# Softmax attention: biased scores moved from PSUM to rows in SBUF, one exponential for a token tile, and another split of the PSUM banks

## The chip, the cores and the metric

The kernel runs on one core of one Trainium2 chip. The metric is the device time of one execution in microseconds (us), the median over runs. Five engines matter: TensorE (PE in the profile; PEld is its weight load), VectorE (DVE), ScalarE (ACT), GpSimd (POOL) and SyncE (SP, which only issues DMAs). PE writes its results into PSUM, which has eight banks of 128 x 512 four-byte values; DVE and ACT read and write PSUM and SBUF.

## The reference, cut to what matters

A network of two layers. Each layer normalises its input, multiplies it with one wide matrix, and gives part of the columns to gated linear attention (GLA, four heads) and part to softmax attention with a forget gate (FoX, eight heads of width 64). The two outputs are normalised by head, joined, multiplied by an output matrix and added to the input; a gated feed-forward network with a short convolution follows. Sequence: 16 learned tokens and 1024 others, 1040 in all. All is float32. FoX is what the change touches:

```python
c = jnp.cumsum(log_f, axis=1)
logits = (jnp.einsum('bqhd,bkhd->bhqk', q_b, kf)
          + c_b[..., None] - c_k[:, :, None, :])
logits = jnp.where(key_pos[None, :] <= q_pos[:, None], logits, -jnp.inf)
return jnp.einsum('bhqk,bkhd->bqhd', jax.nn.softmax(logits, axis=-1), vf)
...
o_fox = rms_norm(o_fox, fox_norm[i].reshape(FOX_HEADS, FOX_DH)).reshape(B, L, FOX_WIDTH)
h = h + jnp.concatenate([o_gla, o_fox], axis=-1) @ w_out[i]
```

## The kernel before

**Numbers in two halves.** Matrix products of full precision are made of three products of a short format: each operand is split into `hi` (a cast on ACT) and `lo` (the rest, a subtraction on DVE, or on POOL for weights). So each product of a layer's weights appears as `mm<-xh,hi`, `mm<-xh,lo`, `mm<-xl,hi` (L221 to L223), and `split` (L332) is an ACT cast at L335 followed by a DVE subtraction at L336.

**FoX.** The 1040 tokens make nine token tiles: tile 0 of 112 tokens, the others of 116. The eight heads are worked through as four pairs p, two heads e in each; for each pair the tiles come in five groups (7,8), (5,6), (3,4), (1,2), (0), for each group both heads, for each head the later tile first. That gives 72 steps in a layer. A step's work for one token tile i and one head is:

- `fox_scores` (L642): the keys up to the tile's end come in chunks of 460, 464 and 116 (`SCORES`). For each chunk PE makes the scores into a PSUM tile `S` by two matmuls (L657, L658). DVE adds the bias row `cb` in place in PSUM and keeps a running minimum `m` (the instruction and its read of the accumulator, both L660; the sign is turned, so that the minimum is the softmax's maximum). When all chunks are there, ACT makes the exponential of each chunk from PSUM into an SBUF tile `P` (`Ps` for the third chunk) at L672, with a sum by row into `d3`; DVE adds the sums to `den` (L676).
- `fox_transposes` (L679), two steps later: PE transposes P tile by tile, up to four into one PSUM tile `tr` (L693; for the third chunk into a bank of `S`, L686), and `split` brings it to SBUF as `PT`, hi and lo. `PT0`, `PT1` and `PT2` stand for the three chunks; there is one buffer of each.
- `fox_av`, three steps later: PE multiplies values by `PT` into the PSUM tile `av` (L711), which ACT copies to SBUF (L714, `avs`).
- `fox_fold` (L716), four steps later: PE transposes `avs` into `fo`, a bank of `S` (L724). ACT and DVE add hi and lo to `ff` (L727, L728), ACT squares it into the SBUF tile `fon` (L730), DVE sums the squares (L734) and multiplies the rows by the inverse root (L739).
- `fox_store` (L743), six steps later: PE transposes the result into a bank of `S` (L750); ACT scales it to SBUF (L757), from where a DMA takes it away. For the last pair it is split into the operand of the output product.

Between these PE runs fill work: the products of the next pair's queries, keys and values, and gates, one accumulator (`mm`) after the other, with ACT and DVE work behind it (L571 to L630). In the last pair the fill work is the output product of the layer.

**Order.** Each engine runs one list in order. A scheduler sets the lists from the source's order, priorities (scores come with a priority of 8) and estimated times; an instruction that waits holds all behind it on its engine. PSUM banks are given out by tag, in turn: `mm` 2, `S` 3, `tr` 2, `av` 1 (L875). A bank is given to the next user of its tag when the last reader of the one before is through.

`head` (L352) makes a layer's first products before anything else fills `mm`; its five accumulators go in turn to the tags `mm, mm, S, S, S` (L355).

Of the kernel before, what the change touches and what calls it, by code (L numbers as in the profile page):

```python
# [10 lines left out]
F32 = mybir.dt.float32  # L11
F32R = mybir.dt.float32r
BF16 = mybir.dt.bfloat16
AF = mybir.ActivationFunctionType
# [22 lines left out]
P_BUFS = 5  # L37
# [97 lines left out]
class Kern:  # L135
# [216 lines left out]
    def head(self, tiles, pp, nm, feed):  # L352
        s = self.slots
        held, w, waiting = [], [], []
        tags = ("mm", "mm", "S", "S", "S")  # L355
        i = 0
# [285 lines left out]
    def fox_scores(self, e, i, q, cb, den, ap, pp):  # L642


        nc = self.nc
        rows = self.rows_of(i)
        kend = self.start_of(i) + rows
        qs = slice(kend - rows, kend)
        m = ap.tile([128, 3], F32, tag="m", name="m", bufs=4)
        Ss = []  # L650
        for c0, n in SCORES:
            if c0 >= kend:
                break
            k1 = min(c0 + n, kend)
            n = k1 - c0
            S = pp.tile([128, 512], F32, tag="S", name="S")
            nc.tensor.matmul(S[:rows, :n], q["qA"][e][:, qs], q["kA"][e][:, c0:k1], start=True, stop=False)  # L657
            nc.tensor.matmul(S[:rows, :n], q["qA"][e][:, qs], q["kL"][e][:, c0:k1], start=False, stop=True)  # L658
            ci = len(Ss)
            nc.vector.tensor_tensor_reduce(out=S[:rows, :n], in0=S[:rows, :n], in1=cb[:rows, c0:k1],  # L660
                                           scale=1.0, scalar=(BIG if ci == 0 else m[:rows, ci - 1:ci]),
                                           op0=ALU.add, op1=ALU.min, accum_out=m[:rows, ci:ci + 1])
            Ss.append((S, n))
        nch = len(Ss)
        Ps = []
        d3 = den if nch == 1 else ap.tile([128, 3], F32, tag="d3", name="d3", bufs=4)
        for ci, (S, n) in enumerate(Ss):
            if ci < 2:
                P = ap.tile([128, 4 * FT], F32, tag="P", name="P", bufs=P_BUFS)
            else:  # L670
                P = ap.tile([FT, FT], F32, tag="Ps", name="Ps", bufs=2)
            nc.scalar.activation(P[:rows, :n], S[:rows, :n], AF.Exp, scale=-1.0, bias=m[:rows, nch - 1:nch],  # L672
                                 accum_out=(den if nch == 1 else d3[:rows, ci:ci + 1]))
            Ps.append(P)
        if nch > 1:
            nc.vector.tensor_reduce(out=den, in_=d3[:rows, :nch], axis=AX.X, op=ALU.add)  # L676
        return Ps

    def fox_transposes(self, i, ci, P, PT, qoff, pp):  # L679
# [3 lines left out]
        tr = pp.tile([128, 4, 128], F32, tag="S" if ci == 2 else "tr", name="tr")  # L683
# [6 lines left out]
        for j in range(nt):  # L690
            t = 4 * ci + j
            o, w = self.start_of(t) - self.start_of(4 * ci), FT if i else FIRST
            nc.tensor.transpose(tr[:w, j, :rows], P[:rows, o:o + w], id_)  # L693
# [22 lines left out]
    def fox_fold(self, tiles, avs, den, ap, pp):  # L716
# [3 lines left out]
        fo = pp.tile([128, 2, 2, 2, 64], F32, tag="S", name="fo")  # L720
# [8 lines left out]
        on = sq = ap.tile([128, 2, 2, 64], F32, tag="fon", name="fon", bufs=1)  # L729
        nc.scalar.activation(sq[:rows, :nt], f[:rows, :nt], AF.Square)  # L730
        vv, d2, y0, a = (ap.tile([128, 2, 2], F32, tag=f"f{x}", name=f"f{x}", bufs=2)[:rows, :nt] for x in "vdya")
# [9 lines left out]
        return on  # L741
# [961 lines left out]
```

## Time and profile before

| what | value |
|---|---|
| three runs | 2593.61, 2605.56, 2600.95 us (median 2600.95) |
| span of the profiled execution | 2598.6 us |
| busy: PE / DVE / ACT / POOL | 2505.2 / 1782.3 / 1281.9 / 430.0 us |
| share of the span | 96% / 69% / 49% / 17% |
| FoX stage of layer 0, of layer 1 | about 181 to 530 us, about 1458 to 1820 us |
| exponentials L672 into P, into Ps | 224 and 16 instructions |
| scores L660 on DVE | 240 instructions and 240 reads of the accumulator |

The profiled execution has no time of its own beside its span; the span is what the profile's windows add up to. Times inside the trace are counted from the span's start. A row of waits reads: who waited, for whom, in total (us), how often, the longest. A row of the timeline reads: start, duration, engine, line, operation, output and inputs, shape, and in brackets the idle time before it with what ended it. A row of windows reads: stretch, length, busy time and count of PE, PEld, DVE, ACT and POOL, then the granted clock of PE (1.00 is full), the share of DMA and the rate.

### The profile page before, as it was taken

How to read it: one execution, taken by the hardware profiler on the slowest of the kernel's cores; microseconds unless marked ns; L12 is line 12 of the kernel's file. 1: busy time of each engine (PE TensorE's matmuls, PEld its weight loads, DVE VectorE, ACT ScalarE, POOL GpSimd, SP SyncE). 2: the span in 40 equal slices, each digit the busy share in tenths (PEclk: the TensorE clock that was granted, in tenths of full speed). 3: DMA queues.
4: the chain of work that ended last, by engine and by line, in shares of the span. 5: the costliest groups of instructions: out<-in, count | busy, mean ns of one | idle time of the engine just before them, and what ended most of it. 6: DMA issues, size and time to landing. Idle time of an engine off the chain costs nothing.

```text
span 2598.6 us, 48715 instructions
## 1 busy us (share of the span) xinstructions
PE 2505.2 (96%) x19278; PEld 2432.4 (94%) x19278; DVE 1782.3 (69%) x3486; ACT 1281.9 (49%) x2737; POOL 430.0 (17%) x598
## 2 busy tenths in 40 slices
PE   8999999899999999999999999998999999999997
PEld 7988999898999999999999899997999999999997
DVE  7656776759877777853665666776698777777535
ACT  7336666535544445641443466665454444455312
POOL 4033334310000000100201233332100000001002
PEclk9999999999999999999999999999999999999999
DMA  3132134333322223763312222142523222247621
GB/s 125 66 86 57 54 93 127 103 121 100 110 75 82 79 82 129 198 160 113 106 53 66 72 78 71 61 142 91 157 62 115 82 78 74 85 157 185 188 66 69
DMA packets 118517, 260.93 MB, mean 100 GB/s; under 512 B 14880, under 2 KB 32544, under 8 KB 118288
## 3 DMA queue, kind: packets, MB, share of 16 engines
q1 hardware_dynamic: 93984, 182.79, 22.4%
q0 software_dynamic: 22432, 72.71, 10.1%
q8 instruction: 151, 2.47, 0.4%
q10 hardware_dynamic: 1872, 2.31, 0.3%
q14 instruction: 78, 0.64, 0.1%
HBM read 177.16 MB, written 67.81 MB: 94 GB/s over the span
## 4 chain that ended last, share of the span: by engine, by line
PE 60%; issue 17%; DVE 14%; ACT 5%; DMA 2%; POOL 1%; SPq 0%; DVEq 0%; POOLq 0%; ACTq 0%
PE mm L221 6%; PE mm L222 6%; PE mm L223 6%; PE up L221 5%; PE up L223 5%; PE up L222 5%; PE down L221 5%; PE down L222 5%; PE down L223 5%; PE av L711 2%; DVE S L660 2%; PE tr L693 2%; ACT P L672 1%; DVE PT L336 1%; PE S L657 1%
## 5 line engine op out<-in xcount | busy, mean ns | idle before, releaser
L221 PE MATMUL up<-x,hi 128*128 128x260 f32 (+1 forms) x2464 | 700.0, 284 | 2.4 <-ACT x L1050 2.4
L223 PE MATMUL up<-x,hi 128*128 128x260 f32 (+1 forms) x2464 | 698.9, 284 | 1.9 <-DVE x L1051 1.8
L222 PE MATMUL up<-x,lo 128*128 128x260 f32 (+1 forms) x2464 | 698.6, 284 | 0.0
L223 PEld LDWEIGHTS up<-x,hi 128*128 128x128 f32 x2464 | 468.2, 190 | 3.4 <-DVE x L1051 3.4
L221 PEld LDWEIGHTS up<-x,hi 128*128 128x128 f32 x2464 | 467.4, 190 | 3.5 <-ACT x L1050 3.2
L222 PEld LDWEIGHTS up<-x,lo 128*128 128x128 f32 x2464 | 467.5, 190 | 0.2 <-DVE lo L1027 0.2
L1027 DVE TENSOR_TENSOR lo<-raw,hi 128x512 fp32r<-128x512 f32 x364 | 248.8, 688 | 171.8 <-ACT hi L1026 171.8
L221 PE MATMUL mm<-xh,hi 128*128 128x348 f32 (+4 forms) x1056 | 365.5, 346 | 0.0
L223 PE MATMUL mm<-xl,hi 128*128 128x348 f32 (+4 forms) x1056 | 341.3, 323 | 0.0
L222 PE MATMUL mm<-xh,lo 128*128 128x348 f32 (+4 forms) x1056 | 340.1, 322 | 0.0
L1026 ACT CAST hi<-raw 128x512 fp32r<-128x512 f32 x364 | 224.4, 621 | 138.5 <-PE up L223 93.5
L221 PEld LDWEIGHTS mm<-xh,hi 128*128 128x128 f32 x1056 | 201.0, 190 | 5.8 <-issue 5.3
L188 ACT CAST hi<-raw 128x512 fp32r<-128x512 f32 (+2 forms) x184 | 107.4, 587 | 200.7 <-PE down L223 116.2
L222 PEld LDWEIGHTS mm<-xh,lo 128*128 128x128 f32 x1056 | 200.9, 190 | 0.4 <-issue 0.3
L223 PEld LDWEIGHTS mm<-xl,hi 128*128 128x128 f32 x1056 | 199.8, 189 | 0.3 <-issue 0.3
L222 PE MATMUL down<-ah,lo 128*128 128x260 f32 (+1 forms) x704 | 198.6, 282 | 0.4 <-DVE lo L190 0.3
L223 PE MATMUL down<-al,hi 128*128 128x260 f32 (+1 forms) x704 | 198.4, 282 | 0.0
L221 PE MATMUL down<-ah,hi 128*128 128x260 f32 (+1 forms) x704 | 198.1, 281 | 0.0
L672 ACT ACTIVATE P<-S,m 116x460 f32<-116x460 f32 (+2 forms) x224 | 124.8, 561 | 103.9 <-DVE m L660 101.5
L336 DVE TENSOR_TENSOR PT<-tr,PT 116x464 fp32r<-116x464 f32 (+3 forms) x240 | 123.0, 516 | 63.8 <-ACT PT L335 62.9
L1235 POOL DMA_DIRECT2D actd<-cv x44 | 23.6, 536 | 763.7 <-DVE cv L1234 742.8
L1009 DVE TENSOR_TENSOR raw<-raw,raw 128x512 f32<-128x512 f32 x198 | 129.8, 689 | 19.7 <-DMA raw<-in_wd_dram 17.2
(277 smaller groups left out, 5889.6 us busy)
## 6 DMA issues: line engine op xcount, KB each, us to landing
raw<-in_wm_dram SPq DMA_DIRECT2D x330, 256.0 KB, 2.8
raw<-in_wd_dram SPq DMA_DIRECT2D x64, 256.0 KB, 3.5
actd<-cv POOLq DMA_DIRECT2D x22, 520.0 KB, 3.0
actd<-cv POOLq DMA_DIRECT2D x22, 512.0 KB, 3.0
cb<-cd SPq DMA_DIRECT2D x16, 520.0 KB, 4.0
st<-actd SPq DMA_DIRECT2D x14, 520.0 KB, 4.6
st<-actd SPq DMA_DIRECT2D x14, 512.0 KB, 5.2
kA<-kA SPq DMA_DIRECT2D x24, 260.0 KB, 4.3
```

The source lines that it names most:

```text
L188: nc.scalar.copy(hi[:, :n, :], raw[:, :n, :])
L221: nc.tensor.matmul(ps, wh, xh[:, c0:c0 + n], start=first, stop=False, skip_group_check=more)
L222: nc.tensor.matmul(ps, wl, xh[:, c0:c0 + n], start=False, stop=False, skip_group_check=more)
L223: nc.tensor.matmul(ps, wh, xl[:, c0:c0 + n], start=False, stop=last, skip_group_check=more)
L336: nc.vector.tensor_tensor(out=lo, in0=src, in1=hi.bitcast(F32), op=ALU.subtract)
L660: nc.vector.tensor_tensor_reduce(out=S[:rows, :n], in0=S[:rows, :n], in1=cb[:rows, c0:k1], scale=1.0, scalar=(BIG if ci == 0 else m[:rows, ...
L672: nc.scalar.activation(P[:rows, :n], S[:rows, :n], AF.Exp, scale=-1.0, bias=m[:rows, nch - 1:nch], accum_out=(den if nch == 1 else d3[:row ...
L693: nc.tensor.transpose(tr[:w, j, :rows], P[:rows, o:o + w], id_)
L711: nc.tensor.matmul(av[:, a:width], w.rearrange("p a b -> p (a b)"), x, start=(t == 0 and i == 0), stop=(t == last and i == 1))
L1009: nc.vector.tensor_tensor(out=q[out][:, :nk, :], in0=q[a][:, :nk, :], in1=q[b][:, :nk, :], op=op)
L1026: nc.scalar.copy(hi[:, :nk, :], src[:, :nk, :])
L1027: nc.vector.tensor_tensor(out=lo[:, :nk, :], in0=src[:, :nk, :], in1=hi[:, :nk, :].bitcast(F32), op=ALU.subtract)
```

## The change

DVE now writes the biased scores of a chunk not back to PSUM but into a row in SBUF: `P` is one tile of 924 columns (`LOW`) for the first two chunks, `Ps` one of 116 for the third. ACT then makes one exponential in place over the row's first part, at most 924 wide, and one over `Ps` where there is one. Sums of two parts are added by one DVE instruction, only for rows of three chunks. A bank of `S` is free once DVE is through, and no longer once ACT is. The tags have other banks: `S` 2 in place of 3, `tr` 3 in place of 2. `fo`, the transposes of `fox_store` and those of `Ps` take a bank of `tr` in place of one of `S`; `head` takes its five accumulators in the order `mm, S, mm, S, tr`. The squares go to the half of `fo`'s bank that has been read, and the product with the inverse root is made in place in `ff`, so that the tile `fon` is gone. Line numbers after the change are one or two higher.

```diff
-P_BUFS = 5
+LOW = 924
+P_BUFS = 3
...
-        tags = ("mm", "mm", "S", "S", "S")
+        tags = ("mm", "S", "mm", "S", "tr")
...
-            nc.vector.tensor_tensor_reduce(out=S[:rows, :n], in0=S[:rows, :n], in1=cb[:rows, c0:k1],
+            ci = len(Ps)
+            if ci == 0:
+                P = ap.tile([128, LOW], F32, tag="P", name="P", bufs=P_BUFS)
+            elif ci == 2:
+                P = ap.tile([FT, FT], F32, tag="Ps", name="Ps", bufs=2)
+            x = P[:rows, c0:k1] if ci < 2 else P[:rows, :n]
+            nc.vector.tensor_tensor_reduce(out=x, in0=S[:rows, :n], in1=cb[:rows, c0:k1],
                                            scale=1.0, scalar=(BIG if ci == 0 else m[:rows, ci - 1:ci]),
                                            op0=ALU.add, op1=ALU.min, accum_out=m[:rows, ci:ci + 1])
-            Ss.append((S, n))
-        nch = len(Ss)
-        Ps = []
-        d3 = den if nch == 1 else ap.tile([128, 3], F32, tag="d3", name="d3", bufs=4)
-        for ci, (S, n) in enumerate(Ss):
-            if ci < 2:
-                P = ap.tile([128, 4 * FT], F32, tag="P", name="P", bufs=P_BUFS)
-            else:
-                P = ap.tile([FT, FT], F32, tag="Ps", name="Ps", bufs=2)
-            nc.scalar.activation(P[:rows, :n], S[:rows, :n], AF.Exp, scale=-1.0, bias=m[:rows, nch - 1:nch],
-                                 accum_out=(den if nch == 1 else d3[:rows, ci:ci + 1]))
             Ps.append(P)
-        if nch > 1:
-            nc.vector.tensor_reduce(out=den, in_=d3[:rows, :nch], axis=AX.X, op=ALU.add)
+        nch = len(Ps)
+        low = m[:rows, nch - 1:nch]
+        d2 = ap.tile([128, 2], F32, tag="d2", name="d2", bufs=2) if nch == 3 else None
+        x = Ps[0][:rows, :min(kend, LOW)]
+        nc.scalar.activation(x, x, AF.Exp, scale=-1.0, bias=low, accum_out=(den if nch < 3 else d2[:rows, 0:1]))
+        if nch == 3:
+            x = Ps[2][:rows, :rows]
+            nc.scalar.activation(x, x, AF.Exp, scale=-1.0, bias=low, accum_out=d2[:rows, 1:2])
+            nc.vector.tensor_tensor(out=den, in0=d2[:rows, 0:1], in1=d2[:rows, 1:2], op=ALU.add)
...
-        tr = pp.tile([128, 4, 128], F32, tag="S" if ci == 2 else "tr", name="tr")
+        tr = pp.tile([128, 4, 128], F32, tag="tr", name="tr")
...
-        fo = pp.tile([128, 2, 2, 2, 64], F32, tag="S", name="fo")
+        fo = pp.tile([128, 2, 2, 2, 64], F32, tag="tr", name="fo")
...
-        on = sq = ap.tile([128, 2, 2, 64], F32, tag="fon", name="fon", bufs=1)
+        sq = fo[:, :, :, 0]
...
-            nc.vector.tensor_tensor(out=on[:rows, ti], in0=f[:rows, ti],
+            nc.vector.tensor_tensor(out=f[:rows, ti], in0=f[:rows, ti],
...
-        tr = pp.tile([128, 4, 128], F32, tag="S", name="tr")
+        tr = pp.tile([128, 4, 128], F32, tag="tr", name="tr")
...
-            pp = PsumTags({"mm": (pp2, 2), "S": (pp1, 3), "tr": (pp2, 2), "av": (pp1, 1)})
+            pp = PsumTags({"mm": (pp2, 2), "S": (pp1, 2), "tr": (pp2, 3), "av": (pp1, 1)})
```

The scheduler makes new lists out of this. In most places a list reads as before and only what is waited for differs. Three places follow; the prediction calls them A, B and C. All three are in layer 0, pair 1, and recur in the other pairs. The bracket at a row's end names the engine whose semaphore the row waits for; what it stands for is told with each. `kA`, `kL` and `qA` are the keys (hi, lo) and the queries of a head.

**Place A**, PE, the first row of a pair, with its three chunks. Before:

```order
L657 MATMUL S<-kA_2370,qA_2368 116x460 [waits DMAHW1_49]
L693 MATMUL tr<-ident,P 112x112 [waits PE_49]
L658 MATMUL S<-kL_2372,qA_2368 116x460 [waits DMAHW3_49]
L657 MATMUL S<-kA_2370,qA_2368 116x464
L658 MATMUL S<-kL_2372,qA_2368 116x464 [waits Pool_49]
L657 MATMUL S<-kA_2370,qA_2368 116x116 [waits Activation_49]
L658 MATMUL S<-kL_2372,qA_2368 116x116
L221 MATMUL mm<-xh_138,hi 128x344
L222 MATMUL mm<-xh_138,lo 128x344
L223 MATMUL mm<-xl_139,hi 128x344
```

And after the change:

```order
L658 MATMUL S<-kA_2358,qA_2356 116x460 [waits DMAHW1_49]
L695 MATMUL tr<-ident,P 112x112 [waits PE_49]
L659 MATMUL S<-kL_2360,qA_2356 116x460 [waits DMAHW3_49]
L658 MATMUL S<-kA_2358,qA_2356 116x464
L659 MATMUL S<-kL_2360,qA_2356 116x464 [waits Pool_49]
L222 MATMUL mm<-xh_138,hi 128x344
L223 MATMUL mm<-xh_138,lo 128x344
L224 MATMUL mm<-xl_139,hi 128x344
L658 MATMUL S<-kA_2358,qA_2356 116x116 [waits DVE_49]
L659 MATMUL S<-kL_2360,qA_2356 116x116
```

The third chunk's matmul has moved behind three `mm`. It waited for ACT to be through with a bank that `fox_store` had used; it now waits for DVE to be through with the first chunk of the same row, the one just made, since there are two banks.

**Place B**, PE, the second row of tile group (5,6). Before:

```order
L657 MATMUL S<-kA_2370,qA_2368 116x460 [waits Activation_49]
L222 MATMUL mm<-xh_142,lo 128x344
L658 MATMUL S<-kL_2372,qA_2368 116x460
L223 MATMUL mm<-xl_143,hi 128x344
L693 MATMUL tr<-ident,P 116x116 [waits DVE_49]
L657 MATMUL S<-kA_2370,qA_2368 116x232 [waits Activation_49]
```

And after the change:

```order
L658 MATMUL S<-kA_2358,qA_2356 116x460 [waits DVE_49]
L223 MATMUL mm<-xh_142,lo 128x344
L659 MATMUL S<-kL_2360,qA_2356 116x460
L224 MATMUL mm<-xl_143,hi 128x344
L695 MATMUL tr<-ident,P 116x116 [waits DVE_49]
L658 MATMUL S<-kA_2358,qA_2356 116x232
```

The order stands. The first `S` waited for the exponential of the row before (its first chunk); it now waits for DVE's bias instruction on that chunk. The `tr` waits in both for the DVE subtraction that makes `PT0` out of the `tr` bank it takes. On ACT, at the same place, before:

```order
L623 ACTIVATE gy<-gy 128x348
L335 CAST PT_3572<-tr 116x4x116
L672 ACTIVATE P,d_3592<-S,m 116x460
L672 ACTIVATE P,d_3592<-S,m 116x348
L335 CAST PT_3573<-tr 116x4x116
L714 COPY avs<-av 128x232
```

And after the change:

```order
L624 ACTIVATE gy<-gy 128x348
L336 CAST PT_3519<-tr 116x4x116
L674 ACTIVATE P,den<-P,m 116x808
L336 CAST PT_3520<-tr 116x4x116
L716 COPY avs<-av 128x232
```

The exponential over 460 and the one over 348 stand as one over 808, between the same two casts.

**Place C**, PE, the second row of tile group (1,2). Before:

```order
L223 MATMUL mm<-xl_147,hi 128x348
L657 MATMUL S<-kA_2370,qA_2368 116x228 [waits Activation_49]
L658 MATMUL S<-kL_2372,qA_2368 116x228
L693 MATMUL tr<-ident,P 116x116 [waits DVE_49]
L693 MATMUL tr<-ident,P 116x116 x3
L221 MATMUL mm<-xh_132,hi 128x344
```

And after the change:

```order
L224 MATMUL mm<-xl_147,hi 128x348
L658 MATMUL S<-kA_2358,qA_2356 116x228
L659 MATMUL S<-kL_2360,qA_2356 116x228
L695 MATMUL tr<-ident,P 116x116 [waits DVE_49,PE_49]
L695 MATMUL tr<-ident,P 116x116 x3
L222 MATMUL mm<-xh_132,hi 128x344
```

The order stands here too. `S` has no wait left. The first `tr` waited for the DVE subtraction that empties the `tr` bank of two uses before into `PT0`; with three banks it takes the bank that `fo` had, and waits for DVE's sum of squares (L734 before, L736 after).

More of the change, by code (lines that the diff above doesn't have):

```diff
@@ L649, in fox_scores @@
         m = ap.tile([128, 3], F32, tag="m", name="m", bufs=4)
-        Ss = []
+        Ps = []
         for c0, n in SCORES:
@@ L691, in fox_transposes @@
             t = 4 * ci + j
-            o, w = self.start_of(t) - self.start_of(4 * ci), FT if i else FIRST
+            o, w = self.start_of(t), FT if i else FIRST
             nc.tensor.transpose(tr[:w, j, :rows], P[:rows, o:o + w], id_)
@@ L728, in fox_fold @@
         nc.vector.tensor_tensor(out=f[:rows, :nt], in0=fo[:rows, :nt, :, 1], in1=f[:rows, :nt], op=ALU.add)
-        on = sq = ap.tile([128, 2, 2, 64], F32, tag="fon", name="fon", bufs=1)
+        sq = fo[:, :, :, 0]
         nc.scalar.activation(sq[:rows, :nt], f[:rows, :nt], AF.Square)
-        vv, d2, y0, a = (ap.tile([128, 2, 2], F32, tag=f"f{x}", name=f"f{x}", bufs=2)[:rows, :nt] for x in "vdya")
+        vv, d2, y0, a = (ap.tile([128, 2, 2], F32, tag=f"f{x}", name=f"f{x}", bufs=1)[:rows, :nt] for x in "vdya")
         nc.vector.scalar_tensor_tensor(out=d2, in0=den[:rows, :nt], scalar=64.0 * EPS,
```

3 lines of the change are left out of this document (1 added, 2 removed).

## Prediction

> **What bounds the kernel now.** I read the page first (busy time by engine, chain by engine), then windows by stage, then what PE waited for in the two stages that the change touches.
>
> ```profile
> PE 2505.2 (96%) x19278; PEld 2432.4 (94%) x19278; DVE 1782.3 (69%) x3486; ACT 1281.9 (49%) x2737; POOL 430.0 (17%) x598
> ...
> PE 60%; issue 17%; DVE 14%; ACT 5%; DMA 2%; POOL 1%; SPq 0%; DVEq 0%; POOLq 0%; ACTq 0%
> ```
>
> PE is busy for 96% of the span and carries most of the chain. The change takes no matmul away. So it can win only idle time of PE, and only where the waiting is for something that the change touches: a bank of scores or of transposes.
>
> ```profile
> 180.00:540.00 360.00, 334.97 (x2306) 318.45 (x2306) 242.09 (x750) 216.48 (x650) 124.45 (x176) 0.99 0.28 84
> ```
>
> The windows by stage give 360 - 335 = 25 us of idle PE in the stage of softmax attention of layer 0. The waits of PE say for what; the first fence is layer 0, the second the same stage of layer 1.
>
> ```profile
> PE tr L693 <- DVE PT L336: 9.2, 8, 2.2
> PE S L657 <- ACT P L672: 5.5, 5, 1.5
> PE mm L221 <- ACT hi L188: 2.9, 2, 2.7
> PE mm L222 <- POOL lo L190: 2.5, 4, 1.0
> ```
>
> ```profile
> PE tr L693 <- DVE PT L336: 7.8, 7, 2.2
> PE S L657 <- ACT P L672: 5.1, 5, 1.3
> ```
>
> Two rows are of the kind that the change acts on. A transpose waits until DVE has emptied a bank of `tr`; scores wait until ACT's exponential has emptied a bank of `S`. Together 14.7 us in layer 0 and 12.9 in layer 1, 27.6 us in all: the ceiling of what can be won, 1.06% of the time. The rows below them (weights cast by ACT, split by POOL) are left as they are.
>
> **The change part by part.**
>
> *The bias instruction on DVE writes SBUF.* 240 instructions, as many as before. The trace has none that writes this way; the nearest is the subtraction L336, which also reads PSUM and SBUF and writes SBUF.
>
> ```profile
> L660 DVE CUSTOM_DVE_ANT_0 S<-S,cb x144: 272/635/679, 188.3 to 1802.2; 116x460 f32<-116x460 f32 x96, 116x344 f32<-116x344 f32 x16, 116x228 f32<-116x228 f32 x16, 112x112 f32<-112x112 f32 x16
> ...
> L336 DVE TENSOR_TENSOR PT<-tr,PT x240: 264/631/643, 195.5 to 1809.9; 116x464 fp32r<-116x464 f32 x82, 116x348 fp32r<-116x348 f32 x16, 116x116 fp32r<-116x116 f32 x14, 112x112 fp32r<-112x112 f32 x8
> ```
>
> Minimum, median and maximum in ns: 635 for the one and 631 for the other, both mostly at 460 or 464 columns. I take no difference; the bounds are -0.05 and +0.05 us each, 12 us of DVE in all, of which little reaches PE, since DVE is busy for 242 of the 360 us.
>
> *One exponential for two.* The 240 exponentials become 160. The new one reads and writes SBUF and is up to 924 wide. The trace has ACT work from SBUF to SBUF at 348 and 1040 columns.
>
> ```profile
> L672 ACT ACTIVATE P<-S,m x224: 347/639/666, 191.4 to 1802.6; 116x460 f32<-116x460 f32 x80, 116x344 f32<-116x344 f32 x16, 116x116 f32<-116x116 f32 x8, 112x112 f32<-112x112 f32 x8
> ...
> L621 ACT ACTIVATE ge<-ge x24: 491/495/521, 265.8 to 1759.0; 128x348 f32<-128x348 f32 x16, 128x344 f32<-128x344 f32 x8
> ...
> L335 ACT CAST x<-st x24: 1037/1056/1087, 1040.8 to 2367.0; 128x1040 fp32r<-128x1040 f32 x12, 128x1024 fp32r<-128x1024 f32 x12
> ```
>
> A line through 495 ns at 348 and 1056 at 1040 rises by 0.811 ns a column: 0.868 us at 808, 0.962 at 924. The pair of exponentials over 460 and 348 (next fence) holds ACT from 285.78 until the next cast starts at 286.93, 1.15 us. The single one would hold it for about 0.87, so it saves some 0.28, and 80 of these 22 us. Bounds: nothing (if the exponential is as much dearer than a cast as 639 ns at 460 columns is against 586 on my line, 0.05 us, and its sum is read out on top) and 30 us. ACT is busy for 216 of the 360 us and is waited for by PE only through the banks, so I count none of it by itself.
>
> [...]
>
> *Place B: scores no longer wait for the exponential.* The timeline of pair 1, layer 0:
>
> ```profile
> 285.06 0.32 PE L221 MATMUL mm<-xh,hi 128*128 128x344 f32 x1
> 286.57 0.47 PE L657 MATMUL S<-kA,qA 128*116 128x460 f32 x1 [1.19 <-ACT P L672]
> ...
> 287.40 0.26 PE L693 MATMUL tr<-ident,P 116*116 116x116 f32 x1
> ...
> 285.78 0.65 ACT L672 ACTIVATE P<-S,m 116x460 f32<-116x460 f32 x1
> ...
> 286.93 0.55 ACT L335 CAST PT<-tr 116x464 fp32r<-116x464 f32 x1
> ...
> 284.64 0.14 DVE L660 DVE_READ_ACCUMULATOR2_ANT m<- 116x1 f32 x1
> ...
> 285.91 0.64 DVE L336 TENSOR_TENSOR PT<-tr,PT 116x464 fp32r<-116x464 f32 x1
> ...
> 456.14 0.47 PE L657 MATMUL S<-kA,qA 128*116 128x460 f32 x1 [1.31 <-ACT P L672]
> ```
>
> PE stood for 1.19 us until the exponential was through. DVE was through with that bank at 284.78, before PE wanted it, so this stall goes. But the `tr` three rows further waits, before and after, for the subtraction that ends at 285.91 + 0.64 = 286.55. It starts there and not at 287.40: net gain 0.85 us of 1.19. The place comes in pairs 1, 2 and 3 (the last at 456.14): 3 x 0.85 = 2.55.
>
> *Place C: a third bank of transposes.* The same pair, and the same place in pair 2:
>
> ```profile
> 325.71 0.61 PE L693 MATMUL tr<-ident,P 116*116 116x116 f32 x4 [1.36 <-DVE PT L336]
> ...
> 329.14 0.57 PE L711 MATMUL av<-PT,V 112*128 112x232 f32 x3
> ...
> 327.65 0.64 DVE L336 TENSOR_TENSOR PT<-tr,PT 116x464 fp32r<-116x464 f32 x1 [0.63 <-ACT PT L335]
> ...
> 321.18 0.42 DVE L734 TENSOR_REDUCE fv<-fon 116x4 f32<-116x256 f32 x1 [0.48 <-ACT fon L730]
> ...
> 410.35 0.32 PE L693 MATMUL tr<-ident,P 116*116 116x116 f32 x1 [1.37 <-DVE PT L336]
> ```
>
> The transposes now take the bank that `fo` had, free since the sum of squares at 321.60, so the 1.36 us go. PE would reach the next `av` at 329.14 - 1.36 = 327.78. That `av` needs `PT0`, which DVE finishes at 327.65 + 0.64 = 328.29 by a chain (exponential of 344 columns, cast, subtraction) that the change does not shorten. So `av` is late next: the gain is 329.14 - 328.29 = 0.85. Pairs 0, 1 and 2: 2.55.
>
> *Pair 3.* Here the fill work is the output product, whose operands DVE and ACT split.
>
> ```profile
> 482.64 1.95 DVE L336 TENSOR_TENSOR ml<-h,mh 128x384 fp32r<-128x384 f32 x4
> ...
> 486.30 0.63 DVE L336 TENSOR_TENSOR PT<-tr,PT 116x464 fp32r<-116x464 f32 x1
> ...
> 481.81 0.61 PE L693 MATMUL tr<-ident,P 116*116 116x116 f32 x4 [2.20 <-DVE PT L336]
> ...
> 485.07 0.41 PE L693 MATMUL tr<-ident,P 116*116 116x116 f32 x2 [1.38 <-DVE PT L336]
> ...
> 486.99 0.38 PE L711 MATMUL av<-PT,V 112*128 112x232 f32 x1 [0.33 <-DVE PT L336]
> ```
>
> The 2.20 and the 1.38 us go, but the `av` at 486.99 waited for DVE already, which works through splits without a pause. PE comes earlier to the same wait. I take 0.5 us, between nothing and their sum.
>
> *The rest of a layer*: pair 0's start and some small waits, 14.7 - 3.75 (B) - 4.1 (C) - 3.6 (pair 3), with 1.25 for B as the mean of the two rows shown, 1.37 for C, and 2.20 + 1.38 for pair 3. That leaves 3.3 us, where the order is rearranged most. I take 0.6, between -2 and +2.
>
> *Place A: a wait is added.* The third chunk's scores now wait for DVE's work on the first chunk of their own row; queued behind them on PE are the fill products and all transposes.
>
> ```profile
> 261.66 0.21 PE L657 MATMUL S<-kA,qA 128*116 128x116 f32 x1
> ...
> 261.82 0.38 PE L221 MATMUL mm<-xh,hi 128*128 128x344 f32 x1
> ...
> 262.34 0.32 PE L221 MATMUL mm<-xh,hi 128*128 128x344 f32 x1
> ...
> 261.44 0.65 DVE L660 CUSTOM_DVE_ANT_0 S<-S,cb 116x460 f32<-116x460 f32 x1 [1.11 <-PE S L658]
> 262.00 0.14 DVE L660 DVE_READ_ACCUMULATOR2_ANT m<- 116x1 f32 x1
> ```
>
> Three `mm` (261.82 to 262.34, 0.52 us) now stand ahead, so PE would come at about 261.66 + 0.52 = 262.18; DVE is through at 262.14. I cost it at nothing. The cover is 0.04 us, though: whatever delays DVE here delays PE by as much.
>
> *`fo`, stores and `Ps` in banks of `tr`, squares in PSUM, shorter sums:* nothing; their waits lie several fill products behind their producers. Bounds of -1 and +1 us a layer.
>
> Sum for a layer: 2.55 + 2.55 + 0.5 + 0.6 = 6.2 us. Layer 1 shows nearly the same waits: 12.4 us, off the profiled span of 2598.6 about 2586. The span is 2.35 us below the median of the runs shown; against the median I take the same difference: 2601 - 12 = **2589 us**.
>
> **The rivals.**
>
> *All of the waits go* (2573 us). Then `PT`'s chain would have to move ahead with PE. For it: with three banks a cast has more to choose from, and shorter exponentials let ACT come sooner. Against it: at B and C the next wait is in the trace. Price: 27.6 us, 2601 - 27.6.
>
> *The waits only change their name* (2600 us). Three more users crowd the three banks of `tr`, and `PT0`, with its one buffer, is waited for in any case. For it: 0.34 us of B and 0.5 of C come back already on paper, and pair 3 keeps nearly all. Against it: 0.85 us remain at six places. Price: 0 to 3 us gained.
>
> *Scores hold PE* (2614 us, slower). PE's list is in order. With two banks each chunk's scores need DVE to be through two chunks back, and at place A the margin is 0.04 us. If DVE has other things ahead there, say one subtraction of 0.64 us with one bias instruction of 0.63, PE stands for 1.3 us at the 16 rows with three chunks (there are 16 `Ps`), 21 us, which leaves 12.4 - 21 = 8.6 us lost. Against it: in pair 1 DVE had stood idle for 1.11 us before, waiting for PE. A pause may also cost speed:
>
> ```profile
> 180.00:184.00 4.00, 2.24 (x14) 1.78 (x14) 3.91 (x10) 1.20 (x4) 2.51 (x2) 1.00 0.19 68
> 184.00:188.00 4.00, 4.00 (x19) 3.76 (x19) 1.17 (x4) 2.03 (x7) 1.10 (x2) 0.57 0.70 217
> ...
> 324.00:328.00 4.00, 2.64 (x19) 2.46 (x19) 2.07 (x6) 3.75 (x11) 2.81 (x3) 1.00 0.04 4
> ```
>
> After 4 us with 2.24 of PE's work the granted clock was 0.57 for the next 4; after 2.64 at place C (a stall as it is now) the row has 1.00. So a stretch like the first costs (1 - 0.57) x 4 = 1.7 us more. Three or four of the 16 rows falling into it give 2601 + 8.6 + 5 = 2614. It decides from 12.4 / 16 = 0.8 us a row (no gain left) and from 25.4 / 16 = 1.6 us a row, the clock included, it is slower by over 0.5%. [...]
>
> **How the numbers follow.** Forecast (waits of B and C, less what comes back, 2582 to 2596) 0.45; all go 0.18; names only 0.22; scores hold PE 0.15. A measurement tells 0.5%, 13 us, from no change, and the forecast of 12 lies at that line: of its 0.45 I put 0.22 beyond it. Faster: 0.22 + 0.18 = 0.40. Of the slower rival 0.12 is beyond the line on the other side; the same: 0.23 + 0.22 + 0.03 = 0.48. The range runs from the ceiling of what can be won, 2573, to 2608, which cuts the slower rival's larger half.
>
> **What would show it.** Right: the row of scores waiting for the exponential is gone, transposes waiting for `PT` fall to about 4 us a layer, and `av` waiting for `PT` rises by some 2 us; idle PE in the window of 360 us falls from 25 to about 19. Wrong: waits of scores for DVE of more than 3 us a layer (rival three), `tr` waiting for `fo` or the store (rival two), or a bias instruction clearly above 0.64 us.

## The result

| kernel | median of runs | range | span of the profiled execution |
|---|---|---|---|
| before | 2603.26 us (4 runs) | 2593.61 to 2606.36 | 2598.6 us |
| changed | 2591.23 us (4 runs) | 2589.74 to 2591.80 | 2589.8 us |

The ratio is 0.9955, 95% interval 0.9934 to 0.9976: 12 us faster. That interval reaches from 6 to 17 us. The change was timed twice more, with ratios of 0.9962 (0.9950 to 0.9974) and 0.9965 (0.9953 to 0.9977), which is 9 us each time.

The page of the changed kernel, busy time and chain by engine, and the row of windows for the attention stage of layer 0 (PE busy second after the length):

```profile
PE 2503.3 (97%) x19278; PEld 2431.3 (94%) x19278; DVE 1770.5 (68%) x3422; ACT 1267.7 (49%) x2577; POOL 428.3 (17%) x598
...
PE 54%; issue 23%; DVE 12%; ACT 4%; DMA 4%; POOL 2%; SPq 0%; DVEq 0%; POOLq 0%; ACTq 0%
```

```profile
180.00:540.00 360.00, 341.42 (x2350) 325.96 (x2349) 240.03 (x728) 212.89 (x580) 123.73 (x176) 0.99 0.29 86
```

Idle PE in that window fell from 25.0 to 18.6 us. What PE waited for there (total, times, longest):

```profile
PE tr L695 <- DVE PT L337: 5.2, 5, 2.1
...
PE S L658 <- DVE m L666: 2.5, 6, 0.8
PE mm L224 <- DVE ml L337: 2.2, 2, 1.2
PE tr L545 <- DVE on L538: 1.5, 2, 1.0
...
PE av L713 <- DVE PT L337: 0.5, 2, 0.3
```

And in layer 1:

```profile
PE tr L695 <- DVE PT L337: 4.8, 5, 2.1
...
PE mm L224 <- DVE ml L337: 2.2, 2, 1.2
...
PE S L658 <- DVE m L666: 1.9, 5, 0.7
```

No scores wait for an exponential any more (5.5 and 5.1 us before). Transposes wait for 4.0 and 3.0 us less. Two rows are larger or new: scores now wait for DVE's bias instruction, 2.5 and 1.9 us, and products of the last pair wait 2.2 us for `ml`, 0.5 before.

To compare kernels whose lists differ, lengths were taken from the traces' PE records between matmuls that every kernel has: the time from the last score matmul of the pair before (the one of 112 x 112) to that of pair 1 and of pair 3, and the attention part of a layer, from its first `z` (a product of the gated linear attention) to the first `up` of the feed-forward network. The attention part thus holds the gated linear attention as well as FoX.

```
                 pair 1, layer 0 / 1     pair 3, layer 0 / 1     attention part, layer 0 / 1
before           84.23 / 84.30           94.58 / 93.20           549.95 / 548.76
before again     84.24 / 84.51           95.02 / 92.97           547.09 / 548.69
changed          82.20 / 82.14           95.85 / 93.73           541.39 / 541.80
changed again    82.34 / 82.05           95.25 / 93.04           541.00 / 541.03
changed, third   82.30 / 82.07           94.97 / 95.47           541.68 / 544.86
rows only        84.96 / 83.10           96.29 / 93.87           547.32 / 544.23
banks only       83.08 / 83.15           96.79 / 94.58           548.37 / 553.37
two exponentials 82.94 / 82.72           94.02 / 94.08           540.57 / 544.33
```

Profiles of one kernel agree to 0.2 us in pair 1, but differ by up to 2.4 us in pair 3 and by up to 3.8 in the attention part. The last section shows one cause. The mean of both layers together is 1097.2 us before (two profiles) and 1083.9 with the change (three): 13.3 us won there. The rest of the spans took a mean of 1502.1 us before and 1504.6 with the change; the two profiles of the kernel before differ by 4.4 us there, so this is no finding.

### The profile page after: what moved, and what is told of

The parts are those of the page before. It is cut to its first block, busy times and chain, and to the rows that moved or that the text cites. A ratio compares the mean times of both kernels' runs of the same rounds, so it can differ in the third digit from the quotient of the medians.

```text
span 2589.8 us, 48526 instructions
## 1 busy us (share of the span) xinstructions
PE 2503.3 (97%) x19278; PEld 2431.3 (94%) x19278; DVE 1770.5 (68%) x3422; ACT 1267.7 (49%) x2577; POOL 428.3 (17%) x598
## 4 chain that ended last, share of the span: by engine, by line
PE 54%; issue 23%; DVE 12%; ACT 4%; DMA 4%; POOL 2%; SPq 0%; DVEq 0%; POOLq 0%; ACTq 0%
PE mm L222 6%; PE mm L223 6%; PE mm L224 6%; PE down L222 5%; PE down L223 5%; PE down L224 5%; PE up L224 4%; PE up L223 4%; PE up L222 4%; PE av L713 2%; PE tr L695 2%; DVE P L666 1%; PE S L658 1%; DVE lo L1029 1%; PE S L659 1%
## 5 line engine op out<-in xcount | busy, mean ns | idle before, releaser
L674 ACT ACTIVATE P<-P,m 116x924 f32<-116x924 f32 (+4 forms) x144 | 110.4, 767 | 99.8 <-DVE m L666 96.4
```

The lines of the kernel that those rows point to most:

```text
L674: nc.scalar.activation(x, x, AF.Exp, scale=-1.0, bias=low, accum_out=(den if nch < 3 else d2[:rows, 0:1]))
```

## The experiments

There were three sets. In each, four kernels and the kernel before ran side by side on one chip. "Ratio" is to that kernel, with its 95% interval. The waits and lengths of a kernel come from one profile, where nothing else is said.

**The two kernels again.** The kernel before and the changed one, without an edit.

> The kernel before once more, for a second profile. If waits follow from the order of the lists, its two rows of waits (9.2 and 5.5 us in layer 0, 7.8 and 5.1 in layer 1) come out within 1 us, while the stages that the change leaves alone (GLA, feed-forward) move by up to 3 us with where the half-speed stretches fall. If not, the waits move as well, by over 1 us.

> The changed kernel once more, for a second profile and a time on the same chip as the three kernels beside it. Theory M (waits of places B and C removed, about 6 us a layer): ratio to the kernel before 0.9955 +- 0.001, the waits of scores for DVE and of transposes for PT within 0.5 us of the first profile's 2.5 and 5.2 us a layer, since they follow from the order of the lists. Rival R2 (the gain is chance, from where PE's half-speed stretches of 3.4 us fall): the waits move by over 1 us a layer, the ratio may lie anywhere between 0.993 and 1.000, and the stretches fall at other places.

> The changed kernel again, to be timed in the same rounds as the three kernels beside it. Expected by all theories: ratio to the kernel before 0.9945 to 0.9970, waits in the attention stages as before within 0.8 us a layer, the wait of 2.0 us for h at the start of layer 1.

Measured: the kernel before 0.9992 (0.9977 to 1.0008) against itself, the changed one 0.9962 and 0.9965. The waits of the kernel before, in its second profile, layer 0 and then layer 1:

```profile
PE tr L693 <- DVE PT L336: 8.1, 8, 2.2
PE S L657 <- ACT P L672: 6.0, 5, 1.7
```

```profile
PE tr L693 <- DVE PT L336: 8.3, 8, 2.2
PE S L657 <- ACT P L672: 5.3, 5, 1.5
```

Waits of scores repeat to 0.5 us, those of transposes to 1.1, a little more than expected. The changed kernel's were 5.5, 3.5, 4.0 and 4.7 us for transposes in two further profiles (layer 0 and layer 1 of each) and 1.7, 1.9, 2.4 and 2.3 for scores. They moved by up to 1.3 us, more than the two expectations allowed and, for one row, more than the 1 us that was to speak for chance. The gain itself came back both times, and pair 1 repeats to 0.2 us, so chance does not make the gain. But a single row of waits is good to about 1.5 us, and a difference below that needs pair 1 or the times.

**Only the rows.** Rows in SBUF and the single exponential, but three banks for scores, two for transposes, and all users where they were:

```diff
-        tags = ("mm", "S", "mm", "S", "tr")
+        tags = ("mm", "mm", "S", "S", "S")
-        tr = pp.tile([128, 4, 128], F32, tag="tr", name="tr")
+        tr = pp.tile([128, 4, 128], F32, tag="S" if ci == 2 else "tr", name="tr")
-        fo = pp.tile([128, 2, 2, 2, 64], F32, tag="tr", name="fo")
+        fo = pp.tile([128, 2, 2, 2, 64], F32, tag="S", name="fo")
-        tr = pp.tile([128, 4, 128], F32, tag="tr", name="tr")
+        tr = pp.tile([128, 4, 128], F32, tag="S", name="tr")
-            pp = PsumTags({"mm": (pp2, 2), "S": (pp1, 2), "tr": (pp2, 3), "av": (pp1, 1)})
+            pp = PsumTags({"mm": (pp2, 2), "S": (pp1, 3), "tr": (pp2, 2), "av": (pp1, 1)})
```

> Only the rows in SBUF and the single exponential; the banks and their users as before (S 3, tr 2). Theory M: the waits of scores for ACT's exponential go, those of transposes for PT stay at 8 to 9.5 us a layer; the gain is B's half, 2.5 to 4 us a layer, so 5 to 8 us in all, ratio 0.997 to 0.998. Rival R1 (what counts is the shorter work of ACT, not the banks): the whole gain is there, ratio 0.9955, and the waits of transposes fall to 5 us a layer as well.

Measured: ratio 0.9968 (0.9956 to 0.9980). Its waits in layer 0:

```profile
PE tr L695 <- DVE PT L337: 8.6, 8, 1.8
PE S L658 <- DVE m L666: 4.0, 5, 1.6
```

The waits go with theory M: those for the exponential are gone (scores wait 4.0 us for DVE in their place, 1.4 in layer 1), the transposes wait as before. By the attention parts of this one profile the rows win 5.7 us of the 13.3 (1091.55 against 1097.25), and pair 1 loses 0.7 us in layer 0 and gains 1.3 in layer 1, where the full change gains 2.0 and 2.3. The time says something else: it lies just below M's range of ratios, and with a median of 2593.63 us, beside 2592.78 for the changed kernel and 2601.83 for the one before in the same rounds, the rows alone have 8 of the 9 us. Outside the attention parts this profile is 4.5 us shorter than the mean of the changed kernel's, 1.6 of it at `head` (below). So the rows alone bring part of the gain; how large a part is open.

**Only the banks.** The scores in place in PSUM and an exponential for each chunk, as before, with the new banks. The third chunk's scores take a bank of `tr`:

```diff
+            S = pp.tile([128, 512], F32, tag="tr" if c0 == 924 else "S", name="S")
```

> Only the banks: S 2, tr 3, with the scores in place in PSUM and one exponential for each chunk, as before. The third chunk's scores take a bank of tr, since with two banks of S they could never get one before the exponentials, which need all three chunks' minimum. Theory M: the two banks of S are free only after the exponentials of the whole row, so the next row's scores wait for them; from a bias instruction's end to its exponential's end lie 1.2 to 2 us at 64 rows of two or more chunks in a layer, half of it under fill work: waits of scores for ACT of 15 to 60 us a layer and a time 1 to 4% above the kernel before. Rival R1': with fewer stalls of transposes it comes out about equal to the kernel before, ratio 0.997 to 1.003.

Measured: ratio 1.0034 (1.0021 to 1.0047), 9 us slower than before. Waits in layer 0:

```profile
PE S L657 <- ACT P L672: 10.4, 9, 2.8
...
PE tr L693 <- DVE PT L336: 1.7, 1, 1.7
```

The direction is M's, the size is not: 10 us a layer and not 15 to 60. With the run before it this takes the change apart. The third bank of transposes takes their waits from 9.2 to 1.7 us, and the bank it is taken from costs scores 5 us more as long as it is ACT that frees a bank of scores. The rows take that cost away: with both, the scores wait 2.5 and 1.9 us. The 9 us are not explained by these two rows, which together fell by 2.6 us in layer 0. In the two attention parts PE is idle for 3.6 us less than before (51.9 against a mean of 55.5), but busy for 8 us longer (1049.9 against 1041.7) with the same matmuls. Half speed, as in the last section, would do that (the mean granted clock of this profile is 0.987, beside 0.990 and 0.991 in the two of the kernel before); how much of the 9 us it is, and what the third chunk's place in `tr` and the order in `head` add, was not taken apart.

**Two exponentials.** The changed kernel with an exponential for each chunk, in place in the row:

```diff
+        for ci in range(nch):
+            c0, n = SCORES[ci]
+            n = min(n, kend - c0)
+            x = Ps[ci][:rows, c0:c0 + n] if ci < 2 else Ps[ci][:rows, :n]
+            nc.scalar.activation(x, x, AF.Exp, scale=-1.0, bias=low, accum_out=(den if nch == 1 else d3[:rows, ci:ci + 1]))
```

> The changed kernel with one exponential for each chunk again, in place in the SBUF row (240 in place of 160), and their sums added on DVE as before; m with three buffers in place of four. Theory M (the single exponential is worth little): within 0.15% of the changed kernel, ACT busy 15 to 25 us longer, waits of transposes for PT at most 1 us a layer longer. Rival R1 (shorter ACT work brings the gain): half or more of the gain is lost, ratio to the kernel before 0.998 to 1.000.

Measured: ratio 0.9969 (0.9957 to 0.9980), beside 0.9962 for the changed kernel in the same rounds. Busy time of the page: ACT 1285.1 us, where the changed kernel has 1267.7. Pair 1 is 0.6 us longer than the changed kernel's; pair 3 of layer 0 is 1.4 us shorter, and the two attention parts together take 1084.9 us, beside 1083.9. So the merged exponential saves ACT 17 us, of which PE gains nothing that the times or the attention parts can tell. Rival R1 falls: most of the gain is still there.

**The order in head.**

```diff
-        tags = ("mm", "S", "mm", "S", "tr")
+        tags = ("mm", "mm", "S", "S", "tr")
```

> The changed kernel with head's accumulators in the order mm, mm, S, S, tr in place of mm, S, mm, S, tr. Theory H (the order in head costs what the profile shows at the start of layer 1: a wait of 2.0 us of an mm for DVE's last addition to h at L1553, which the kernel before does not have): that wait falls to about 0.5 us, the time falls by 1 to 2 us, the attention stages stay within 1 us. Rival (which bank head takes does not matter, the wait follows from where the layer before ends): the wait stays at 2 us.

> The changed kernel with head's order mm, mm, S, S, tr, for a time in the same rounds as the changed kernel. Theory H (2.00 us of waiting become 0.44): 1 to 3 us faster than the changed kernel, the difference within what such rounds can tell; the start of layer 1 from the down projection's first matmul to the first z comes out 1 to 2 us shorter. Rival (the faster median of the first look was the draw of the half-speed stretches): no difference in the median, although the wait is gone.

Measured: ratio 0.9944 (0.9927 to 0.9962) and 0.9945 (0.9933 to 0.9957); in the second set the median is 2587.58 us, beside 2592.97 for the changed kernel. The waits at the start of layer 1, changed kernel and then this one:

```profile
PE mm L222 <- DVE h L1553: 2.0, 1, 2.0
```

```profile
PE mm L223 <- DVE wl L191: 0.4, 1, 0.4
```

In the changed kernel the second accumulator takes a bank that the feed-forward network's last addition still reads. The other order takes that bank later. The wait of 2.0 us is in every profile with the change's order (also in the one with banks only) and in none with the other. From the first `down` to the first `z` the program takes 284.95, 284.31 and 284.42 us in the three profiles of the changed kernel, 283.32 and 283.07 in these two: 1.4 us less. (The kernel before, without the wait, took 283.15 and 286.49, so this length alone would not show it.) Both medians are the lowest of the study, and the second is 5.4 us below the changed kernel in the same rounds, more than the 1 to 3 that were expected. The wait explains 1.6 of it. The attention parts, which were expected to stay, are 1.0 us shorter in layer 0 and 3.2 in layer 1 (means, 540.4 and 539.3 against 541.4 and 542.6); why is not known.

**The last pair's weights on DVE.** The first two lower halves of the output weights made on DVE and not on POOL:

```diff
+                        self.att = False
                         ready = self.weights(self.wm[lyr, M_WO])
+                        self.att = True
```

> The changed kernel, with the lower halves of the first output weights of the last pair made on DVE in place of POOL (two instructions of 128x512 a layer). In the changed kernel's trace DVE's L629 in the last pair takes 1.61 us in place of 0.52 while POOL makes such a half (1.32 us), and PE then waits 0.96 and 1.22 us for ml. Theory P (the two engines hold each other up, and that delay is what PE waits for): L629 takes 0.5 to 0.6 us, the waits for ml fall from 2.2 to under 1 us a layer, the time falls by 2 to 6 us with the half-speed stretch behind them. Rival (DVE is full there anyway): DVE has 2 x 0.69 us more to do, the waits for ml or PT grow by 1 us or more, the time stays or rises by up to 3 us.

Measured: ratio 0.9960 (0.9945 to 0.9975). The changed kernel did not run in this set; beside its 0.9955 to 0.9965 in the others no gain can be told. The changed kernel's timeline in the last pair of layer 0 (start, duration, then what ran):

```profile
465.35 1.61 DVE L629 SCALAR_TENSOR_TENSOR h<-gy,gog 128x348 f32<-128x348 f32 x1
...
465.26 1.32 POOL L191 TENSOR_TENSOR lo<-raw,hi 128x512 fp32r<-128x512 f32 x1 [0.66 <-ACT hi L189]
...
467.98 0.39 PE L224 MATMUL mm<-ml,hi 128*128 128x256 f32 x1 [0.96 <-DVE ml L337]
...
469.82 0.58 PE L224 MATMUL mm<-ml,hi 128*128 128x256 f32 x1 [1.22 <-DVE ml L337]
```

And the edited kernel's:

```profile
465.33 0.52 DVE L629 SCALAR_TENSOR_TENSOR h<-gy,gog 128x348 f32<-128x348 f32 x1
...
466.40 0.69 DVE L191 TENSOR_TENSOR lo<-raw,hi 128x512 fp32r<-128x512 f32 x1
...
471.28 1.35 DVE L626 SCALAR_TENSOR_TENSOR ge<-ge,gy 128x344 f32<-128x344 f32 x1
...
470.95 1.31 POOL L191 TENSOR_TENSOR lo<-raw,hi 128x512 fp32r<-128x512 f32 x1 [0.18 <-ACT hi L189]
```

L629 is back at 0.52 us, so POOL's instruction had held it up. The waits for `ml` fell only to 1.5 and 1.2 us, from 2.2. The next lower half, still on POOL, now meets L626, which takes 1.35 us where its median is 0.52. Theory P is right about the instruction and wrong about the price: what is won in one place is met again a few microseconds on. From 463 to 473 us DVE is busy for all of the 10 us in both traces.

**The third chunk's scores in a bank of transposes.**

```diff
-            S = pp.tile([128, 512], F32, tag="S", name="S")
+            S = pp.tile([128, 512], F32, tag="tr" if c0 == LOW else "S", name="S")
```

> The changed kernel with the third chunk's scores in a bank of tr in place of S, so that they no longer wait for DVE's work on their own row's first chunk. Theory A (this wait, 0.25 to 0.75 us at most rows of three chunks, is paid by PE): waits of scores for DVE fall from 2.5 and 1.9 to under 1 us a layer, the time falls by 1 to 3 us. Rival (it moves into tr): the transposes' waits for PT rise by as much, the time stays within 1 us.

Measured: ratio 0.9971 (0.9960 to 0.9983). Waits in layer 1:

```profile
PE tr L695 <- DVE PT L337: 5.7, 7, 2.1
PE mm L224 <- DVE ml L337: 3.6, 3, 1.4
...
PE av L713 <- DVE PT L337: 2.2, 4, 1.3
...
PE S L658 <- DVE m L666: 0.2, 1, 0.2
```

In layer 1 scores wait 0.2 us, but transposes, `ml` and `av` wait longer. In layer 0 scores still wait 2.1 us, in two places, where under 1 was expected, and transposes 5.6. Nothing is won, and in layer 1 the wait moved, as the rival has it. (The changed kernel did not run in this set.)

**The fold in a bank of scores.** With the other order in head:

```diff
-        fo = pp.tile([128, 2, 2, 2, 64], F32, tag="tr", name="fo")
+        fo = pp.tile([128, 2, 2, 2, 64], F32, tag="S", name="fo")
```

> As the kernel with the other order in head, with fo back in a bank of S, the rest of tr's users as in the change. Theory M (with two banks of S nothing else may live there: fo holds its bank over a copy, an addition, a square and a sum, 1.6 to 2 us): waits of scores for DVE or ACT rise by 4 to 15 us a layer, at 20 folds a layer, ratio to the kernel before 0.998 to 1.006. Rival (the fold is far enough from the next scores): no change within 2 us, and the waits of transposes fall by 1 us a layer as tr has one user less.

Measured: ratio 0.9970 (0.9958 to 0.9981), against 0.9945 with `fo` in `tr`. Waits in layer 0:

```profile
PE S L658 <- DVE fv L736: 4.9, 4, 2.3
PE tr L695 <- DVE PT L337: 4.5, 4, 2.1
```

Scores now wait 4.9 us for the sum of squares, the last reader of `fo`. This is M's mechanism at the lower end of its size, and the ratio just below its range. With two banks of `S`, taking `fo` out of them is worth 8 us (2595.43 against 2587.58).

**Priority for PT.** With the other order in head, and the splits of transposes at the priority of the scores:

```diff
+        with self.tc.high_priority(8):
+            self.split(PT[ci][:w, :nt, 0, qs], PT[ci][:w, :nt, 1, qs], tr[:w, :nt, :rows])
```

> As the kernel with the other order in head, and with the splits of transposes into PT given the same priority of 8 as the scores. Theory C2 (what is left of the transposes' waits, about 5 us a layer, is the place of PT's subtractions behind other DVE work): the waits of transposes and of av for PT fall from 5.5 to under 3 us a layer, the time falls by 3 to 6 us. Rival (DVE and ACT then make something else late): the waits for ml, h and scores rise by as much, the time stays within 2 us or rises.

Measured: ratio 0.9968 (0.9956 to 0.9980), 6 us slower than without it. Waits in layer 1:

```profile
PE tr L695 <- DVE PT L337: 4.1, 5, 2.1
PE mm L224 <- DVE ml L337: 2.6, 2, 2.1
PE av L714 <- DVE PT L337: 2.3, 6, 0.6
PE av L714 <- ACT PT L336: 2.0, 4, 1.0
```

The transposes' wait hardly fell, and `av` waits more, for ACT too. Moving these splits forward in the lists does not remove the waits; whether another order would was not tried.

The best kernel of the study is thus the change with head's other order, at 0.9944 and 0.9945.

## Why the prediction was right, point by point

It forecast 2589 us, 12 less than before; 2591.23 was measured, 12.0 less than the median of the four runs of the kernel before. That the two agree so closely is luck: the interval is 6 to 17 us, two more sets gave 9, and the terms of the sum were mostly off. The table sets them beside the lengths of the profiles (us won, mean of two before less mean of three after):

| stretch of a layer | forecast | layer 0 | layer 1 |
|---|---|---|---|
| first `z` to the end of pair 0 (0.85 for C, 0.6 for "the rest") | 1.45 | 3.6 | 3.9 |
| pair 1 (B and C) | 1.70 | 2.0 | 2.3 |
| pair 2 (B and C) | 1.70 | 2.2 | 0.5 |
| pair 3 (B and "0.5 us") | 1.35 | -0.6 | -1.0 |
| end of pair 3 to the first `up` | 0 | 0.0 | 0.5 |
| sum | 6.2 | 7.2 | 6.2 |

The mechanism holds: what went are waits for a bank of scores or of transposes. Its places were only in part the ones forecast.

**Pair 0, "the rest of a layer"**: the largest miss. Pair 0 was counted with one place C, and what it had besides was part of 3.3 us of waits of which 0.6 were to be won. More of it went. These are PE's waits from the first `z` to the end of pair 0 in layer 0, before and after the change:

```profile
PE tr L693 <- DVE PT L336: 2.7, 3, 1.4
...
PE S L657 <- ACT P L672: 1.5, 2, 1.3
...
PE u L505 <- DVE kd L491: 0.5, 1, 0.5
PE z L461 <- DVE gk L412: 0.2, 1, 0.2
```

```profile
PE tr L695 <- DVE PT L337: 0.9, 1, 0.9
PE u L506 <- DVE kd L492: 0.9, 1, 0.9
PE z L462 <- DVE B L349: 0.8, 1, 0.8
...
PE S L658 <- DVE m L666: 0.2, 1, 0.2
```

Transposes and scores wait 3.1 us less, of which the stall of place C is 1.4. The clock records also have four stretches of half speed there in the four cases before (two layers, two profiles), and one in the six after, which is part of the 3.6 and 3.9 us. The rows also show a cost that had no term: `z` and `u` of the gated linear attention take banks of `S` too, and with two of them they wait 1.0 us longer (0.7 in layer 1). With rows only these two waits are as before (0.5 and 0.2), with banks only as after the change (0.9 and 0.8), so the bank that `S` lost is the cause.

**Bias instruction and exponential.** The two rows of the changed kernel (minimum, median and maximum in ns):

```profile
L666 DVE CUSTOM_DVE_ANT_0 P<-S,cb x144: 262/627/637, 188.2 to 1792.7; 116x460 f32<-116x460 f32 x96, 116x344 f32<-116x344 f32 x16, 116x228 f32<-116x228 f32 x16, 112x112 f32<-112x112 f32 x16
...
L666 DVE DVE_READ_ACCUMULATOR2_ANT m<- x240: 74/83/86, 188.8 to 1792.9; 116x1 f32 x112, 112x1 f32 x8
```

627 ns, 8 less than before; no difference was forecast, with bounds of 50. The read of the accumulator, which was not considered, is 60 ns shorter (142 before). ACT is busy for 14.2 us less (1281.9 to 1267.7), where 22 were forecast. At place B the exponential over 808 columns holds ACT from 364.07 to 365.03 (next fence), 0.96 us and not 0.87.

**Place B**: right at two of its three places in each layer. Here is pair 2 of the changed kernel in layer 0, and behind it pair 3:

```profile
364.07 0.97 ACT L674 ACTIVATE P<-P,m 116x808 f32<-116x808 f32 x1
...
365.03 0.53 ACT L336 CAST PT<-tr 116x464 fp32r<-116x464 f32 x1
...
364.21 0.63 DVE L337 TENSOR_TENSOR PT<-tr,PT 116x464 fp32r<-116x464 f32 x1
...
364.90 0.32 PE L695 MATMUL tr<-ident,P 116*116 116x116 f32 x1 [0.79 <-DVE PT L337]
...
447.52 0.47 PE L658 MATMUL S<-kA,qA 128*116 128x460 f32 x1 [0.78 <-DVE m L666]
```

In pair 2 scores do not wait, and the transpose behind them starts as the subtraction ends (364.84), as forecast. In pair 3 the scores waited 0.78 us for the bias instruction itself: DVE was late there, which the forecast had taken to be through. In layer 1 the same happens in pair 2 (0.67 us) and not in pair 3.

**Place C**: the 1.36 us are gone, as forecast, but the wait of 0.5 us that was to come back at the next `av` is not in the rows. In layer 0 `av` as a whole waits 0.5 us for `PT`, where it waited 1.4 before and some 2 us more were forecast. The kernel shows why: the first `av` matmul reads only the hi half, which the cast makes (through at 322.35 in pair 1); only the second needs the subtraction. That ends at 323.03, the second matmul starts at 323.08, and the row of five takes 1.09 us where it took 0.80 before: so some 0.3 of the 0.5 us are hidden in it. C's term was too small.

**Pair 3** is a step that failed: "I take 0.5 us" won, and 0.85 for B. Pair 3 takes 94.8 us before (mean of two) and 95.4 after (mean of three) in layer 0, 93.1 and 94.1 in layer 1: 0.6 and 1.0 us more. Profiles differ by up to 2.4 us there, so a loss is not shown, only that the gain is missing. A stall of 2.1 us at a transpose remains in four of the six cases (two layers, three profiles), and the products wait 2.2 us for `ml`, since a DVE instruction now meets one of POOL and takes 1.61 us in place of 0.52. The run with the weights on DVE shows that meeting; that DVE's full stretch is what keeps the time from falling is argued from it, not shown alone. Half speed takes its part too: the clock records have three stretches of it in pair 3 in all six cases after the change, and two before (three in one of four cases). At 1.7 us each, an estimate from the last section, that is 0.9 us more in layer 0 and 1.7 in layer 1: enough for the 0.6 and 1.0 us, not for all of the gain that is missing.

**Place A**: forecast as nothing, and in pairs 1 and 2 nothing is seen. But in pair 3 it waits 0.75 us (layer 0), and the pairs' second row of three chunks about 0.27: with B's 0.78 and small ones, 2.5 and 1.9 us a layer in all. At 0.3 us a row this stays below the 0.8 at which the slower rival would have eaten the gain.

**Head** had no term in the sum. Its new order costs 2.00 - 0.45 = 1.55 us of waiting, by the runs with the other order.

So the terms of pair 0 and of C were too small, that of pair 3 was too large, the banks of `z` and `u` and `head` had none, and the misses cancelled. The rival "names only" falls with the attention parts, 13.3 us shorter; "all go" falls with 5 us of transposes' waits left in each layer.

## What to carry to other kernels

When an accumulator bank is in short supply, ask which engine's last read sets it free, and move that read to the engine that is through first: here one bank could change its user only because DVE, and no longer ACT, freed the others. Price such a change as a whole, because one half alone (the banks) cost time and the other brought only part of the gain. List every user of a tag that loses a bank: here `z`, `u` and `head` paid too. At each stall that goes, read in the same trace what is late next: that gave 1.7 us for the two stalls of a pair, and pair 1 gained 2.0 and 2.3. It was wrong in pair 3, where DVE is busy without a pause for 10 us, and for the stalls of pair 0, which were not followed one by one. And when a sum agrees with the measurement, compare its terms as well: here they did not agree.

## What the runs showed of the hardware

**In these traces the clock falls by a fixed grid of windows.** The stretches of half speed (0.50 in the clock records) begin a whole number of 3.413 us apart: in the kernel before 12, 50, 143, 174, 426 windows after its first one. Up to 2560 us each lasts 3.41 or 6.83 us in the first profiles of the two kernels. Whether a window is followed by one at half speed goes with PE's busy time in it. Over the fourteen profiles, from 10 to 2560 us: under 1.5 us, always (94 of 94 windows); 1.5 to 2.0 us, in 45 of 85; 2.0 to 2.3 us, in 6 of 101; above that, in 23 of 10150. Half of 3.413 is 1.7, so by estimate the same pause costs 1.7 us more or nothing, by where it falls. Here is the stall of 2.2 us in pair 3 of layer 0, on each profile's own grid, first the kernel before and then the changed one (PE busy after the length, granted clock third from the end):

```profile
477.90:481.30 3.40, 1.72 (x14) 1.40 (x12) 3.40 (x11) 3.25 (x10) 2.05 (x2) 1.00 0.38 151
481.30:484.70 3.40, 1.88 (x12) 1.63 (x12) 3.40 (x9) 3.00 (x8) 1.22 (x3) 1.00 0.23 80
```

```profile
476.50:479.90 3.40, 1.26 (x9) 1.07 (x8) 3.40 (x9) 1.89 (x6) 1.77 (x4) 1.00 0.53 146
479.90:483.30 3.40, 3.40 (x17) 3.30 (x15) 3.40 (x8) 1.15 (x4) 1.91 (x5) 0.50 0.96 275
```

Before, the pause is shared by two windows of 1.72 and 1.88 us and the clock stays at 1.00; after, it lies in one of 1.26 us, and the next runs at 0.50: 1.26 us of work did not keep the clock up. Where a pause falls on the grid would account for profiles of one kernel that agree in their waits and differ by 3 us in a stage; that it makes the whole spread of the runs was not shown.

**POOL held DVE up** in two instructions in which DVE reads two operands from SBUF: 0.52 us became 1.61 and 1.35 beside POOL's instruction of 1.3 us. The subtraction into PT, which reads one operand from PSUM, kept its length: 18 of those over 464 columns ran beside such an instruction of POOL in the changed kernel's trace, with a median of 634 ns and a maximum of 642, where the maximum of all is 644.
